# Attention of a two-layer model on one core: the rotation's exchanged half is added by an accumulating DMA, one conditioning gate changes its engine, and the stages of the attention layer stand in another order

## The chip, the core and the metric

The kernel runs on one core of one Trainium2 chip. The core has a matrix engine (TensorE, PE), a vector engine (VectorE, DVE), a scalar engine (ScalarE, ACT), a general engine (GpSimd, POOL) and a sync engine (SyncE, SP), each with its own instruction queue, and 16 DMA engines that serve the queues. The metric is the device time of one execution in microseconds (us).

## The reference

A model of depth 2 with width 1024 and 256 tokens. Layer 0 is an HGRN mixer and a feed-forward block, layer 1 the attention that the change is about and a second feed-forward block. Each of the four blocks is conditioned: shift, scale and gate come from a matrix of the conditioning vector `c`.

```python
mods = einsum('bd,lde->lbe', silu(c), ada_w) + ada_b      # 4 blocks: shift, scale, gate
# layer 1, keys and values of 4 heads, in three branches
k_cmp, v_cmp, k_sel, v_sel, k_win, v_win = split(modulate(x, ...) @ w_kv)
kc = rms_norm(compress(k_cmp)); vc = compress(v_cmp)
ks = apply_rope(rms_norm(k_sel), cos, sin); kw = apply_rope(rms_norm(k_win), cos, sin)
# queries of 16 heads
q = rms_norm(h @ w_q); q_rope = apply_rope(q, cos, sin)
...
o = g0 * softmax(q kc) vc + g1 * softmax(q_rope ks, causal) v_sel + g2 * softmax(q_rope kw, causal) v_win
x = x + gate * (o @ w_out)

def apply_rope(x, cos, sin):
    x1, x2 = split(x, 2)
    return concat([x1 * cos - x2 * sin, x2 * cos + x1 * sin])
```

`apply_rope` is the rotation: each half of a head's 64 values is multiplied by the cosine, and the other half, multiplied by the sine, is subtracted or added.

## The kernel before

Activations stand transposed in SBUF: 128 partitions, 8 chunks of the width, 256 tokens. All is kept in 32-bit floats. Weights come in chunks of 1 MB (`raw<-in_w`, on SP's queue, in the order of one list, into a ring of four buffers). ACT casts a chunk to its high half `wh` (L337), DVE subtracts to get the low half `wl` (L341), and PE multiplies three times, high by high, high by low and low by high (L551 to L553, or two wider matmuls at L563 and L564).

The **conditioning** is computed along the way, piece by piece, in one of two manners. By `ada_pe` PE multiplies the chunk with `c` (L445, tiles `adaps...`), ACT copies, PE transposes (L458, `adat`) and DVE adds the bias. Else DVE multiplies a chunk with `c` and sums it (L406, `junk<-raw,crep`, two instructions to a chunk of 1 MB). The tuple `ON_PE` says which pieces PE takes: `s` for shift and scale, `g` for the gate, the digit for the block. `g2` is the gate of the attention layer, `s3` the shift and scale of the block behind it.

The **attention layer**, `nsa` (L1337), runs from about 354 us to 501 us of the profiled execution. It projects keys and values, then walks a list of tokens, `ORDER["nsa"]`, which says in which order the stages are recorded:

- `c` and `x`: compression of keys and values, softmax of that branch. `K`: the split activations `h` for values and keys. `G`: the three gates `G`. `w`: the values `V` of a branch (PE tile `v`).
- `q0` to `q3`: the projection of four query heads each (PE tile `nq`) and their rotation. `R` and `n`: norms of the keys and the queries, and their factors.
- `s0` to `s7`, `attend_scores` (L1585): for one pair of heads PE computes scores (L1598, `s<-KR,QR`), DVE adds the mask and takes the maximum (L1603, eight instructions, `Pt<-s`), scales it (L1608, `nm`), ACT takes the exponentials with their sums (L485, eight instructions, `Pt`), and DVE forms the factor (L1618, `rs`; `cf`) and multiplies (L1626, `Pt<-Pt,cf`, two instructions).
- `v0` to `v7`, `attend_values` (L1629): PE transposes the pair's `Pt` (L1640, twelve, into `ptt`), ACT (L1645) and DVE (L1643) copy it in four pieces to `PT`, PE multiplies it with `V` (L1658, `po`), and ACT and DVE split the result for the next product (L546, L547).
- `a`: one piece of the conditioning that is due.

A scheduler puts the recorded instructions in an order on each engine by priority. `AHEAD` shifts the priority of a token, `PRI` that of a kind of stage. `PTV` says which of a pair's copies DVE takes, `QACT` and `KACT` are bit masks of the chunks of the queries' and the keys' activations that ACT computes instead of DVE. `Pt` has three buffers, the scores' tiles share four.

The **rotation** is done six times: keys of two branches (`k0`, `k1`) and four groups of queries (`q0` to `q3`; `q0` serves the pairs 0 and 1, and so on). `rotate` (L1260) has POOL issue four DMAs of 32 partitions that copy the raw heads `u` with halves exchanged to `us`, and DVE multiply `u` by gain and cosine into `KR` or `QR` (L1268). Later `rotate_end` (L1272) has DVE multiply `us` by the exchanged gain and the sine (L1277) and add it to `KR` or `QR` (L1279). `us` has two buffers.

Of the kernel before, what the change touches and what calls it, by code (L numbers as in the profile page):

```python
# [21 lines left out]
P = 128  # L22
S = 256
# [10 lines left out]
WIDE = ((3, 5, 6, 7, 9, 10, 11, 12, 13, 14, 15, 16, 17, 18, 19, 20), range(NF))  # L34
ROOTED = [("ffn_in0", 2, 1), ("ffn_in0", 3, 0), ("kv", 2, 0), ("kv", 4, 0), ("ffn_in1", 2, 1), ("ffn_in1", 3, 0)]
PTS = 3
QACT, KACT = 79, 184
CSTK = 7
PTV = 2

AHEAD = {'s4': 5, 'v1': 10, 'G': -10, 'v2': 20, 'v3': 5, 'q3': -40, 'v7': -10, 'v6': 30, 'v5': 5, 'c1': -20, 'v4': 40}
PRI = {'gates': -165, 'av': 10, 'res': 120, 'rot': -90, 'fh': -25}
EPS = 1e-6
NEG = -1e30
LEVELS = (1, 2, 4, 8, 16, 32, 64, 128)
# [11 lines left out]
def _ada_g(l):  # L59
# [11 lines left out]
    "hada": [1, 1, 1, 2, 5, 5, 5, 6, 6, 7, 7, 7],  # L71
    "f0": [6, 6, 7, 10, 11, 11, 13, 13, 15, 18, 19, 22, 23, 23, 25, 27, 28, 28, 32, 33],
    "nsa": (
        "q0 K c0 c1 G w0 q1 R n0 s0 q2 q3 x0 w1 s1 s2 v0 v1 n1 a s3 s4 a v2 a a a v3 a x1 s5 a s6 v4 v6 s7 v5 a a v7 a a a"
    ).split(),
    "f1": [13, 15, 23, 31],
}
# [65 lines left out]
def constants():  # L143
    c = np.zeros((P, NCST), np.float32)

    def put(n, a):
        c[:, CST[n][0]:CST[n][1]] = a.reshape(P, -1)

    put("ident", np.eye(P, dtype=np.float32))
    p = np.arange(P)  # L150
    put("bd64", (p[:, None] // 64 == p[None, :] // 64).astype(np.float32) / 64)
    ex = np.arange(0, 64, 2, dtype=np.float32) / np.float32(64)
    inv = np.float32(1) / np.power(np.float64(10000), ex.astype(np.float64)).astype(np.float32)
    ang = (np.arange(S, dtype=np.float32)[:, None] * inv[None, :]).astype(np.float64)
    put("cos", np.cos(ang).astype(np.float32).T[p % 32])
    put("sin", np.sin(ang).astype(np.float32).T[p % 32] * np.where(p % 64 < 32, -1, 1)[:, None].astype(np.float32))
# [46 lines left out]
class K:  # L203
# [1053 lines left out]
        return u, sq  # L1257

    @first("rot")
    def rotate(self, u, gain, swap, kr, name):  # L1260

        nc = self.nc
        us = self.s2.tile([P, 2, S], F32, tag="us", bufs=2, name=f"us{name}")
        for b in range(4):
            d, e = 32 * b, 32 * (b ^ 1)
            nc.gpsimd.dma_start(us[d:d + 32], u[e:e + 32])
        cs = self.c("cos")[:, None, :].to_broadcast([P, 2, S])
        nc.vector.scalar_tensor_tensor(kr, u, gain, cs, op0=ALU.mult, op1=ALU.mult)  # L1268
        self.swapped.append((kr, us, swap))

    @first("rot")
    def rotate_end(self):  # L1272

        nc = self.nc
        sn = self.c("sin")[:, None, :].to_broadcast([P, 2, S])
        for kr, us, swap in self.swapped:
            r = nc.vector.scalar_tensor_tensor(us, us, swap, sn, op0=ALU.mult, op1=ALU.mult)  # L1277
            self.after(r, self.last_wl)
            nc.vector.tensor_tensor(kr, kr, us, op=ALU.add)  # L1279
# [57 lines left out]
    def nsa(self):  # L1337
        nc = self.nc
        with self.tc.tile_pool(name="ns", bufs=1) as sp, self.tc.tile_pool(name="ns2", bufs=2) as s2, \
                ExitStack() as self.late:  # L1340
            self.sp, self.s2 = sp, s2
            self.swapped = []
# [19 lines left out]
            with ExitStack() as early:  # L1362
# [44 lines left out]
                def values(br):
# [376 lines left out]
```

## Time and profile before

| | |
|---|---|
| median of 3 runs | 712.99 us (712.82 to 713.07) |
| profiled execution | 715.08 us |
| its span, first to last instruction | 713.3 us |
| mean granted TensorE clock | 0.995 of full speed |

The page of the profile gives busy time by engine, the chain of work that ended last (followed back from the last instruction to what released each step), and groups of equal instructions with their count, their busy time and the mean of one in ns. Windows give the same busy times for stretches of the span, with the granted clock (PEclk) and the share in which the DMA engines were busy. In a timeline each row is a run of equal instructions: start, length, engine, line, operation, output and inputs, count, and in brackets how long the engine was idle before it and who ended that.

### The profile page before, as it was taken

Reading aid. Unit: us, or ns where it says so; the run is one execution under the profiler, and the core shown is the slowest. Engines: PE = TensorE matmul, PEld = TensorE weight load, DVE = VectorE, ACT = ScalarE, POOL = GpSimd, SP = SyncE. Lnnn points to the kernel's source line nnn. Section 1 sums busy time; section 2 is a strip of 40 time slices with the busy share of each in tenths; the row PEclk is TensorE's granted clock in tenths of the full one; section 3 lists DMA queues with packets and bytes.
Section 4 is the critical chain, followed back from the end, with each engine's and each line's share of the span. In section 5 each row is a group of like instructions: output and inputs, shape, how many; then the busy total and the mean of one; then the engine's idle time right before and its main releaser. Section 6 shows DMA issues by size and latency. Waiting matters only on the chain.

```text
span 713.3 us, 13972 instructions
## 1 busy us (share of the span) xinstructions
PE 702.6 (99%) x5495; PEld 608.9 (85%) x5495; DVE 583.6 (82%) x1210; ACT 428.5 (60%) x849; POOL 12.2 (2%) x29
## 2 busy tenths in 40 slices
PE   8999999999999999999999999999999999999998
PEld 5998987999988888988998986545899888888887
DVE  6896977799999999999697997667989887686651
ACT  4669977667554665644475656658757655654330
POOL 0000000000000000000002121000000000000000
PEclk9999999999999999999999999989999999999999
DMA  8997768635589998987639643347655766564530
GB/s 356 425 425 293 257 269 305 237 138 182 177 349 345 331 325 305 355 345 279 248 116 338 212 143 134 149 178 262 219 186 188 260 244 220 201 259 155 200 125 23
DMA packets 28067, 174.00 MB, mean 244 GB/s; under 512 B 3297, under 2 KB 4705, under 8 KB 8290
## 3 DMA queue, kind: packets, MB, share of 16 engines
q1 hardware_dynamic: 26800, 170.80, 64.1%
q0 software_dynamic: 768, 1.57, 0.8%
q8 instruction: 43, 0.70, 0.4%
q10 hardware_dynamic: 434, 0.74, 0.3%
q14 instruction: 22, 0.18, 0.1%
HBM read 170.48 MB, written 1.05 MB: 240 GB/s over the span
## 4 chain that ended last, share of the span: by engine, by line
PE 88%; ACT 5%; DVE 4%; DMA 3%; issue 0%; SPq 0%; DVEq 0%
PE ffo L563 11%; PE ff L563 9%; PE ffo L564 6%; PE ff L564 5%; ACT Pt L485 3%; PE ff L551 2%; PE ff L553 2%; PE ff L552 2%; PE nso L563 2%; DMA raw<-in_w 2%; PE po L1658 2%; PE adapsss L445 2%; PE ptt L1640 1%; PE hg_g L551 1%; PE hg_i L993 1%; PE s L1598 1%
## 5 line engine op out<-in xcount | busy, mean ns | idle before, releaser
L341 DVE TENSOR_TENSOR wl<-raw,wh 128x1024 fp32r<-128x1024 f32 x193 | 234.5, 1222 | 50.7 <-ACT wh L337 49.6
L337 ACT CAST wh<-raw 128x1024 fp32r<-128x1024 f32 x193 | 200.0, 1049 | 116.3 <-PE ffo L563 37.0
L563 PE MATMUL ffo<-g,wh 128*128 128x512 f32 x330 | 116.0, 394 | 0.0
L563 PE MATMUL ff<-h,wh 128*128 128x512 f32 x280 | 99.9, 395 | 0.0
L564 PE MATMUL ffo<-g,wl 128*128 128x256 f32 x330 | 93.0, 282 | 0.0
L564 PE MATMUL ff<-h,wl 128*128 128x256 f32 x280 | 78.5, 280 | 0.0
L563 PEld LDWEIGHTS ffo<-g,wh 128*128 128x128 f32 x330 | 62.0, 188 | 14.5
L406 DVE CUSTOM_DVE_ANT_0 junk<-raw,crep 128x1024 f32<-128x1024 f32 x60 | 73.2, 1220 | 0.3 <-DMA raw<-in_w 0.2
L563 PEld LDWEIGHTS ff<-h,wh 128*128 128x128 f32 x280 | 52.8, 189 | 12.1 <-DVE h L740 0.2
L564 PEld LDWEIGHTS ffo<-g,wl 128*128 128x128 f32 x330 | 61.9, 188 | 0.0
L564 PEld LDWEIGHTS ff<-h,wl 128*128 128x128 f32 x280 | 52.8, 189 | 0.2
L552 PE MATMUL ff<-h,wh 128*128 128x258 f32 (+1 forms) x144 | 40.5, 283 | 0.0
L553 PE MATMUL ff<-h,wl 128*128 128x258 f32 (+1 forms) x144 | 40.3, 283 | 0.0
L551 PE MATMUL ff<-h,wh 128*128 128x258 f32 (+1 forms) x144 | 40.2, 284 | 0.0
L485 ACT ACTIVATE Pt<-Pt,nm,rq 128x128 f32<-128x128 f32 x64 | 34.2, 539 | 3.6 <-DVE nm L1608 3.6
L802 DVE SCALAR_TENSOR_TENSOR x<-ffo,mod,x 128x256 f32<-128x256 f32 x31 | 14.9, 482 | 16.6 <-PE ffo L564 11.5
L553 PEld LDWEIGHTS ff<-h,wl 128*128 128x128 f32 x144 | 27.2, 190 | 0.0
L552 PEld LDWEIGHTS ff<-h,wh 128*128 128x128 f32 x144 | 27.2, 189 | 0.0
L551 PEld LDWEIGHTS ff<-h,wh 128*128 128x128 f32 x144 | 26.9, 189 | 0.3
L563 PE MATMUL nso<-h,wh 128*128 128x512 f32 x64 | 22.5, 394 | 0.0
L1603 DVE CUSTOM_DVE_ANT_0 Pt<-s,cst 128x128 f32<-128x128 f32 (+1 forms) x64 | 19.4, 353 | 3.5 <-PE s L1598 3.4
L546 ACT CAST g<-fg 128x256 fp32r<-128x256 f32 x44 | 17.8, 405 | 7.0 <-DVE fg L1209 5.6
(499 smaller groups left out, 1799.5 us busy)
## 6 DMA issues: line engine op xcount, KB each, us to landing
raw<-in_w SPq DMA_DIRECT2D x147, 1024.0 KB, 5.3
raw<-in_w SPq DMA_DIRECT2D x11, 512.0 KB, 6.9
rawq<-in_w SPq DMA_DIRECT2D x3, 1024.0 KB, 9.1
rawv<-in_w SPq DMA_DIRECT2D x2, 1024.0 KB, 11.3
w1late<-in_w SPq DMA_DIRECT2D x2, 1024.0 KB, 9.8
x<-in_x SPq DMA_DIRECT2D x2, 512.0 KB, 4.9
rawv<-in_w SPq DMA_DIRECT2D x2, 512.0 KB, 8.2
out<-x SPq DMA_DIRECT2D x8, 128.0 KB, 1.9
```

The costliest lines, as they stand in the source:

```text
L337: r = nc.scalar.copy(wh, u)
L341: r = nc.vector.tensor_tensor(wl, u, wh.bitcast(F32), op=ALU.subtract)
L406: r = nc.vector.tensor_tensor_reduce(out=junk, in0=t[:, h * D:(h + 1) * D], in1=self.crep, scale=1.0, scalar=0.0, op0=ALU.mult, op1=ALU.ad ...
L485: r = nc.scalar.activation(out, in_, func, **kw)
L546: self.nc.scalar.copy(hi, v)
L551: mm(ps, lhsT=wh, rhs=hh, start=first, stop=False)
L552: mm(ps, lhsT=wh, rhs=hl, start=False, stop=False)
L553: return mm(ps, lhsT=wl, rhs=hh, start=False, stop=last)
L563: mm(ps, lhsT=w[k][0], rhs=b, start=k == 0, stop=False)
L564: mm(ps[:, 0], lhsT=w[k][1], rhs=b[:, 0], start=False, stop=k == n - 1)
L802: nc.vector.scalar_tensor_tensor(xn[:, m], p, gate[:, m:m + 1], xn[:, m], op0=ALU.mult, op1=ALU.add)
L1603: nc.vector.tensor_tensor_reduce(out=Pt[half][:, br, o:o + n], in0=ps[half][:, br], in1=cs[:, S - n:], scale=1.0, scalar=-3e38, op0=ALU.ad ...
```

## The change

Four things are changed.

1. The rotation. DVE multiplies the raw heads by gain and sine into `us` first, and by gain and cosine into `KR` or `QR`; then four accumulating DMAs on POOL's queue add `us`, halves exchanged, to `KR` or `QR`. The addition on DVE and `rotate_end` are gone, and the sign of the sine's table is turned.
2. The gate `g2` leaves `ON_PE`: its conditioning is now computed by DVE.
3. `PTV` goes from 2 to 0, so that all copies of the transposed `Pt` are ACT's; `QACT` leaves ACT three chunks instead of five, `KACT` gives it five instead of four.
4. `ORDER["nsa"]`, `AHEAD` and `PRI` have other entries.

```diff
-QACT, KACT = 79, 184
+QACT, KACT = 84, 217
-PTV = 2
+PTV = 0
-AHEAD = {'s4': 5, 'v1': 10, 'G': -10, ...}
-PRI = {'gates': -165, 'av': 10, 'res': 120, 'rot': -90, 'fh': -25}
+AHEAD = {'q3': -55, 'c1': -55, 'v4': 110, ...}
+PRI = {'gates': -150, 'av': 0, 'res': 195, 'rot': -75, 'fh': -25}
-ON_PE = ("s1", "g0", "g2", "s3")
+ON_PE = ("s1", "g0", "s3")
-        "q0 K c0 c1 G w0 q1 R n0 s0 q2 q3 x0 w1 s1 s2 v0 v1 n1 a s3 s4 ..."
+        "c0 K c1 q0 G w0 R q1 n0 q2 s0 s1 w1 x0 s2 q3 n1 a v0 v1 s3 a s4 ..."
-    put("sin", np.sin(ang)... * np.where(p % 64 < 32, -1, 1)[:, None]...)
+    put("sin", np.sin(ang)... * np.where(p % 64 < 32, 1, -1)[:, None]...)
-    def rotate(self, u, gain, swap, kr, name):
+    def rotate(self, u, gain, kr, name):
         nc = self.nc
+        cs, sn = (self.c(n)[:, None, :].to_broadcast([P, 2, S]) for n in ("cos", "sin"))
         us = self.s2.tile([P, 2, S], F32, tag="us", bufs=2, name=f"us{name}")
+        nc.vector.scalar_tensor_tensor(us, u, gain, sn, op0=ALU.mult, op1=ALU.mult)
+        nc.vector.scalar_tensor_tensor(kr, u, gain, cs, op0=ALU.mult, op1=ALU.mult)
         for b in range(4):
             d, e = 32 * b, 32 * (b ^ 1)
-            nc.gpsimd.dma_start(us[d:d + 32], u[e:e + 32])
-        cs = self.c("cos")[:, None, :].to_broadcast([P, 2, S])
-        nc.vector.scalar_tensor_tensor(kr, u, gain, cs, op0=ALU.mult, op1=ALU.mult)
-        self.swapped.append((kr, us, swap))
-    def rotate_end(self):
-        for kr, us, swap in self.swapped:
-            r = nc.vector.scalar_tensor_tensor(us, us, swap, sn, op0=ALU.mult, op1=ALU.mult)
-            self.after(r, self.last_wl)
-            nc.vector.tensor_tensor(kr, kr, us, op=ALU.add)
+            nc.gpsimd.dma_start(kr[d:d + 32], us[e:e + 32], accum_op=ALU.add)
```

In the changed kernel the lines of this layer stand 11 to 14 lower than before (the product with the cosine is L1266, that with the sine L1265, the DMAs L1269, the maximum L1589, the final product L1612).

The order of instructions moves with it. The first place is DVE at the first query rotation, before, from the product with the cosine on; `wl_0_5116` is the low half of the weights of the second query group, `h_4879` the activations of keys and values.

```order
L1268 SCALAR_TENSOR_TENSOR QR<-huq_4869,cols,cst 128x512 [waits Activation_49]
L547 TENSOR_TENSOR hrt<-hrr,hry 128x256 [waits Activation_49]
L341 TENSOR_TENSOR wl_0_5116<-raw_5011,wh_0_5115 128x1024 [waits DMAHW6_49,PE_49,Activation_49]
L537 TENSOR_SCALAR sg<-cmp_4916 128x256 [waits PE_49]
L547 TENSOR_TENSOR h_4879<-t_4880,h_4879 128x256 [waits DMAHW5_49,DMAHW4_49,Activation_49]
```

And the same place now (`usq_5006` is the first query rotation's `us`, `wl_0_5131` and `h_4847` are the weights and activations of the rows above):

```order
L1266 SCALAR_TENSOR_TENSOR QR<-huq_5002,cols,cst 128x512
L528 TENSOR_SCALAR hrt<-hrt 128x256 [waits DVE_49]
L530 TENSOR_TENSOR hrr<-hrt,hry 128x256 [waits DVE_49]
L547 TENSOR_TENSOR hrt<-hrr,hry 128x256 [waits Activation_49]
L1265 SCALAR_TENSOR_TENSOR usq_5006<-huq_5002,cols,cst 128x512 [waits DMASW4_49,DMASW6_49,DMASW2_49,DMASW0_49]
L341 TENSOR_TENSOR wl_0_5131<-raw_4843,wh_0_5130 128x1024 [waits DMAHW6_49,Activation_49]
L547 TENSOR_TENSOR h_4847<-t_4848,h_4847 128x256 [waits DMAHW5_49,DMAHW4_49,Activation_49]
```

The product into `us` has come in ahead of the weights and the splits. It waits for four DMAs of POOL's queue (the DMASW semaphores): its buffer was that of the first keys, whose four DMAs read it.

The second place is PE at the first scores, before. The pair 0 (`s_5225` to `s_5234`) stands alone; the next scores come 88 rows later.

```order
L1598 MATMUL s_5225<-KR,QR 128x256 [waits DVE_49,PE_49]
L1598 MATMUL s_5226<-KR,QR 128x256
L994 MATMUL v_5421<-wl_0_5423,h_4879 128x256
L995 MATMUL v_5421<-wh_0_5422,h_4879 128x256
L1598 MATMUL s_5233<-KR,QR 128x512 [waits PE_49,Activation_49]
L1598 MATMUL s_5234<-KR,QR 128x512 [waits DVE_49,PE_49]
```

Now the scores of the pairs 0 (`s_5291` to `s_5300`) and 1 (`s_5327` on) follow each other:

```order
L1584 MATMUL s_5291<-KR,QR 128x256 [waits DMASW1_49,DMASW2_49,DMASW0_49,DMASW3_49,DVE_49,PE_49]
L1584 MATMUL s_5292<-KR,QR 128x256 [waits DMASW5_49,DMASW6_49,DMASW4_49,DMASW7_49,DMASW3_49,DMASW2_49]
L1584 MATMUL s_5299<-KR,QR 128x512 [waits PE_49,Activation_49]
L1584 MATMUL s_5300<-KR,QR 128x512 [waits DVE_49,PE_49]
L1584 MATMUL s_5327<-KR,QR 128x256 [waits DVE_49,PE_49]
L1584 MATMUL s_5328<-KR,QR 128x256 [waits DVE_49,PE_49]
```

The scores of pair 1 moved up to pair 0, and the first of them wait for the accumulating DMAs instead of for an addition on DVE.

The third place is DVE between the products of the first pairs, now; `Pt_5290` is pair 0, `Pt_5326` pair 1, `raw_5227` a chunk of the weights of the gate `g2`, `css` and `cmx` belong to the compressed branch.

```order
L1612 TENSOR_TENSOR Pt_5290<-Pt_5290,cf 128x2x384
L406 ISA junk,mod_3748<-raw_5227,crep 128x1024 [waits DMAHW3_49]
L406 ISA mod_3748 128x1
L1604 RECIPROCAL rs<-sm 128x8 [waits Activation_49]
L1559 TENSOR_REDUCE cmx<-css 128x16 [waits Activation_49]
L1608 TENSOR_TENSOR cf<-rs,G 128x4 [waits DVE_49]
L1608 TENSOR_TENSOR cf<-rs,G 128x4x2
L1560 RECIPROCAL cmx<-cmx 128x16 [waits DVE_49]
L1612 TENSOR_TENSOR Pt_5326<-Pt_5326,cf 128x2x384 [waits DVE_49]
```

Before, no reduction of the conditioning (L406) stood on DVE in this layer's attention; now eight do, two ahead of the first pair's maximum and six between it and that of the third-last pair.

More of the change, by code (lines that the diff above doesn't have):

```diff
@@ L36 @@
 PTS = 3
-QACT, KACT = 79, 184
+QACT, KACT = 84, 217
 CSTK = 7
-PTV = 2
-AHEAD = {'s4': 5, 'v1': 10, 'G': -10, 'v2': 20, 'v3': 5, 'q3': -40, 'v7': -10, 'v6': 30, 'v5': 5, 'c1': -20, 'v4': 40}
-PRI = {'gates': -165, 'av': 10, 'res': 120, 'rot': -90, 'fh': -25}
+PTV = 0
+AHEAD = {'q3': -55, 'c1': -55, 'v4': 110, 'c0': -70, 's7': 5, 'x1': -35, 's3': 10, 's2': -5, 's0': 60, 'q0': 80, 'w1': -10, 's4': -80, 'v2': -25, 'K': 75, 'R': 60, 'v5': 20, 'v7': -15, 'G': -5}
+PRI = {'gates': -150, 'av': 0, 'res': 195, 'rot': -75, 'fh': -25}
 EPS = 1e-6
@@ L73 @@
     "nsa": (
-        "q0 K c0 c1 G w0 q1 R n0 s0 q2 q3 x0 w1 s1 s2 v0 v1 n1 a s3 s4 a v2 a a a v3 a x1 s5 a s6 v4 v6 s7 v5 a a v7 a a a"
+        "c0 K c1 q0 G w0 R q1 n0 q2 s0 s1 w1 x0 s2 q3 n1 a v0 v1 s3 a s4 a a v2 v3 a x1 s6 s5 a s7 v4 v6 a v5 a v7 a a a a"
     ).split(),
@@ L155, in constants @@
     put("cos", np.cos(ang).astype(np.float32).T[p % 32])
-    put("sin", np.sin(ang).astype(np.float32).T[p % 32] * np.where(p % 64 < 32, -1, 1)[:, None].astype(np.float32))
+    put("sin", np.sin(ang).astype(np.float32).T[p % 32] * np.where(p % 64 < 32, 1, -1)[:, None].astype(np.float32))
     caus = np.zeros((P, 2, P), np.float32)
@@ L1259, in rotate @@
     @first("rot")
-    def rotate(self, u, gain, swap, kr, name):
+    def rotate(self, u, gain, kr, name):
         nc = self.nc
+        cs, sn = (self.c(n)[:, None, :].to_broadcast([P, 2, S]) for n in ("cos", "sin"))
         us = self.s2.tile([P, 2, S], F32, tag="us", bufs=2, name=f"us{name}")
+        nc.vector.scalar_tensor_tensor(us, u, gain, sn, op0=ALU.mult, op1=ALU.mult)
+        nc.vector.scalar_tensor_tensor(kr, u, gain, cs, op0=ALU.mult, op1=ALU.mult)
         for b in range(4):
             d, e = 32 * b, 32 * (b ^ 1)
-            nc.gpsimd.dma_start(us[d:d + 32], u[e:e + 32])
-        cs = self.c("cos")[:, None, :].to_broadcast([P, 2, S])
-        nc.vector.scalar_tensor_tensor(kr, u, gain, cs, op0=ALU.mult, op1=ALU.mult)
-        self.swapped.append((kr, us, swap))
-    @first("rot")
-    def rotate_end(self):
-        nc = self.nc
-        sn = self.c("sin")[:, None, :].to_broadcast([P, 2, S])
-        for kr, us, swap in self.swapped:
-            r = nc.vector.scalar_tensor_tensor(us, us, swap, sn, op0=ALU.mult, op1=ALU.mult)
-            self.after(r, self.last_wl)
-            nc.vector.tensor_tensor(kr, kr, us, op=ALU.add)
-        self.swapped = []
+            nc.gpsimd.dma_start(kr[d:d + 32], us[e:e + 32], accum_op=ALU.add)
     def head_sums(self, pairs):
@@ L1327, in head_mul @@
         nc = self.nc
-        self.rotate_end()
         for i in range(len(pairs)):
@@ L1341, in nsa @@
             self.sp, self.s2 = sp, s2
-            self.swapped = []
             self.PC, self.Pt, self.RQ, self.rq = {}, {}, {}, None
@@ L1384, in nsa @@
                 for br in range(2):
-                    self.rotate(kk[br][0], self.col("k_norm", 1 + br), self.col("k_swap", 1 + br), KR[:, :, br], f"k{br}")
+                    self.rotate(kk[br][0], self.col("k_norm", 1 + br), KR[:, :, br], f"k{br}")
                 ks = [KR[:, :, br] for br in range(2)]
@@ L1398, in query @@
                     qq[i] = self.raw_heads(proj("nq", i, hq), f"q{i}", qd[0][:, i % 2] if i > 1 else None)
-                    self.rotate(qq[i][0], self.col("q_norm"), self.col("q_swap"), self.QR[:, 2 * i:2 * i + 2], f"q{i}")
+                    self.rotate(qq[i][0], self.col("q_norm"), self.QR[:, 2 * i:2 * i + 2], f"q{i}")
                 def query_norm(g):
@@ L1403, in query_norm @@
                     self.QN[g] = [u for u, _ in pairs]
-                    self.rotate_end()
                     self.row_norm(pairs, g)
```

## The prediction

> **What bounds the kernel now.** I read the page first, for the share of each engine and the chain that ended last.
>
> ```profile
> span 713.3 us, 13972 instructions
> PE 702.6 (99%) x5495; PEld 608.9 (85%) x5495; DVE 583.6 (82%) x1210; ACT 428.5 (60%) x849; POOL 12.2 (2%) x29
> PE 88%; ACT 5%; DVE 4%; DMA 3%; issue 0%; SPq 0%; DVEq 0%
> ```
>
> TensorE (PE) carries 88% of the chain; the 12% that other engines carry is the room. The diff begins at the keys' rotation (about 374 us) and ends with the attention layer, so I cut that part with the windows view.
>
> ```profile
> core 0: us, PE busy (x) PEld busy (x) DVE busy (x) ACT busy (x) POOL busy (x), PEclk, DMA share, GB/s
> 392.00:418.50 26.50, 26.42 (x218) 24.74 (x217) 24.76 (x48) 17.40 (x36) 5.88 (x12) 1.00 0.62 219
> 418.50:432.60 14.10, 14.10 (x113) 12.99 (x112) 11.98 (x44) 5.85 (x21) 0.00 (x0) 1.00 0.26 85
> 432.60:450.40 17.80, 17.48 (x151) 9.87 (x148) 12.70 (x52) 12.87 (x43) 1.96 (x4) 1.00 0.53 194
> 450.40:473.20 22.80, 20.47 (x134) 12.21 (x134) 15.13 (x65) 13.40 (x46) 0.00 (x0) 0.85 0.15 53
> 473.20:499.60 26.40, 25.64 (x190) 13.43 (x188) 19.09 (x76) 21.01 (x65) 0.00 (x0) 1.00 0.76 296
> ```
>
> Of 392 to 418.5, PE is busy for 26.42 of 26.50 us: a delay there is not absorbed. From 450.4 to 473.2 it is busy for 20.47 of 22.80 us, at a granted clock of 0.85. Finer windows show where that clock went, and the timeline of PE what came first.
>
> ```profile
> 460.00:465.00 5.00, 2.70 (x21) 2.17 (x20) 4.70 (x12) 5.00 (x21) 0.00 (x0) 0.87 0.53 206
> 465.00:470.00 5.00, 4.97 (x25) 3.32 (x25) 2.90 (x8) 1.78 (x5) 0.00 (x0) 0.50 0.01 3
> 461.96 1.39 PE L1640 MATMUL ptt<-cst,Pt 128*128 128x128 f32 x9 [0.62 <-DVE Pt L1626]
> 465.03 0.90 PE L1640 MATMUL ptt<-cst,Pt 128*128 128x128 f32 x3 [1.68 <-ACT PT L1645]
> ```
>
> PE waits 0.62 us for a product of DVE and 1.68 us for a copy of ACT, and the next 5 us run at half clock. So this middle is bound by the softmax loop of scores (PE), maximum (DVE), exponential (ACT), product (DVE), transposes (PE), copies (ACT). DVE is busy for 11.98 + 12.70 + 15.13 = 39.8 us of the 54.7 between 418.5 and 473.2 and waits for 14.9. The rows behind most of that:
>
> ```profile
> 418.62 0.28 DVE L1603 CUSTOM_DVE_ANT_0 Pt<-s,cst 128x128 f32<-128x128 f32 x1
> 439.84 0.20 DVE L1618 RECIPROCAL rs<-sm 128x8 f32<-128x8 f32 x1 [1.53 <-ACT Pt L485]
> 449.79 0.42 DVE L547 TENSOR_TENSOR h<-po,h 128x256 fp32r<-128x256 f32 x1 [2.53 <-ACT h L546]
> 460.13 0.20 DVE L1618 RECIPROCAL rs<-sm 128x8 f32<-128x8 f32 x1 [2.00 <-ACT Pt L485]
> 469.57 0.42 DVE L547 TENSOR_TENSOR h<-po,h 128x256 fp32r<-128x256 f32 x1 [2.06 <-ACT h L546]
> 473.24 0.29 DVE L1603 CUSTOM_DVE_ANT_0 Pt<-s,cst 128x128 f32<-128x128 f32 x1 [0.20 <-PE s L1598]
> ```
>
> DVE starts the first pair's maximum at 418.62 and the third-last pair's at 473.24; in between it stands still because one pair's exponentials or copies are not done and nothing else is queued ahead.
>
> **The rotation of the keys.** These rows set the cost of the new wait.
>
> ```profile
> 379.76 1.41 DVE L1268 SCALAR_TENSOR_TENSOR KR<-huk,cols,cst 128x512 f32<-128x512 f32 x2
> 386.77 0.42 DVE L547 TENSOR_TENSOR hrt<-hrr,hry 128x256 fp32r<-128x256 f32 x1
> 391.53 1.23 DVE L341 TENSOR_TENSOR wl<-raw,wh 128x1024 fp32r<-128x1024 f32 x1 [4.33 <-ACT wh L337]
> L1266 POOL DMA_DIRECT2D usk<-huk x8: 496/497/628, 374.3 to 381.0; - x8
> DMA to landing us min/median/max: 5.6/6.2/7.0
> DMA to landing us min/median/max: 1.9/2.5/3.1
> ```
>
> (The first landing row is that of the keys' copies, in a stretch full of weight loads; the second is that of the queries' copies, later.) Today the copies depend only on the raw heads. In the changed kernel they come behind DVE's two products, and the third rotation's `us` takes the first one's buffer, so its product on DVE waits for the first keys' four accumulating DMAs. Queued behind it on DVE are the low half of the next query weights (`wl`) and the splits of `h` that PE needs for the values at about 392. Today DVE idles 4.33 us there, until 391.53, and that hides part. The products end at 379.76 + 1.41, plus two more products of 0.70 (1.4) and a neighbour of 0.42 that now stands ahead, so at 383.0. The two keys' DMAs alternate on POOL's queue, so the last of the four is the seventh issue: 7 x 0.497 = 3.5, 386.5. With the keys' landing row, 6.2, it lands at 392.7; the product itself (0.7) ends at 393.4, **1.9 us** behind 391.53. The trace has no accumulating DMA. From below, the queries' 2.5 us gives 0, since the wait then ends inside the idle time; from above, two passes of 6.2 give 12.4 and 8.0 us. I take 6.2, because the transfers are the same 64 KB out of and into SBUF in the same loaded stretch. Below nothing I exclude, since at 391.53 DVE waits for ACT anyway.
>
> A page weighs against that. The Trainium skill, "Collectives: The Full Stack", section "The bandwidth ceiling: the fold count and why AG ≠ RS ≠ AR", says that a DMA that adds needs two reads for each write, and that such a step moved half of what a copying step moved. No row here shows it; by it the landing is nearer to 12.4 and the sum below becomes 714.0. That lies between the second and the third rival, and its chance is in theirs.
>
> **The rest of the rotation.** Six additions on DVE go, and the product with the sine stays.
>
> ```profile
> L1277 DVE SCALAR_TENSOR_TENSOR usq<-usq,cols,cst 128x512 f32<-128x512 f32 x4 | 3.0, 748 | 0.0
> L1279 DVE TENSOR_TENSOR QR<-QR,usq 128x512 f32<-128x512 f32 x4 | 2.8, 688 | 0.0
> ```
>
> That is 6 x 0.69 = 4.1 us of DVE. In 392 to 418.5, by the order of both kernels, two conditioning reductions (2.4), one weight split (1.2) and two early products (1.45) come in, two of the keys' products (1.5) and four additions (2.75) leave: 0.8 us more, into DVE's 1.7 us of slack there, so nothing. The queries' DMAs have 5 us and more before the first scores that read them; at 2.5 us they hide, and if one took 6.2 it would cost about 1.
>
> **The second mixing gate, the copies, the order.**
>
> ```profile
> L445 PE MATMUL adapsg<-raw,c 128*32 128x256 f32 x64 | 4.3, 382 | 0.0
> L406 DVE CUSTOM_DVE_ANT_0 junk<-raw,crep 128x1024 f32<-128x1024 f32 x60 | 73.2, 1220 | 0.3 <-DMA raw<-in_w 0.2
> L1643 DVE COPY PT<-ptt 128x384 f32<-128x384 f32 x8 | 4.4, 552 | 0.0
> L1645 ACT COPY PT<-ptt 128x384 f32<-128x384 f32 x24 | 10.7, 478 | 13.4 <-PE ptt L1640 11.7 <-PE po L1658 1.4
> ```
>
> PE loses 4.3 us of matmuls, DVE gains 8 reductions of 1.22 (9.8 us), and 8 copies go from DVE (4.4 us) to ACT (8 x 0.48 = 3.8). I count between the same two marks, first maximum of the first pair to first maximum of the third-last. There the order gives DVE six of the reductions (+7.3), four copies fewer (-2.2), four rotation steps fewer (-2.9) and one product fewer (-0.95): 39.8 + 1.3 = 41.1 us. The waits were 14.9. A reduction that stands where DVE waited takes its own length out of the wait: 14.9 - 7.3 = 7.6. So the stretch is 48.7 us instead of 54.7, **-6.0**. I take that because one stands right behind the first pair's product and ahead of the second's sums, two behind the second's product, three ahead of the fourth pair's maxima, where the waits of 1.53 to 2.53 us are; and because the changed order computes two pairs' scores ahead of any exponential, so ACT goes from one to the other. The bounds: if all waits re-form, 41.1 + 14.9 gives +1.3; if they fall to 4.9, which is what remains when I walk the changed order with these durations, -8.7.
>
> PE must be able to follow. Between the marks it gives up 4.3 us, idles for 0.00 + 0.32 + 2.33 = 2.65 and loses 3.4 to the clock (0.15 x 22.8), against some 3.3 us of the third shift's matmuls that are moved there: 7 us, enough for 6. Its 4.3 us are not credited again, since most of them run while PE would wait for exponentials. What is late next is PE itself.
>
> **The tail.**
>
> ```profile
> 494.96 1.83 DVE L1626 TENSOR_TENSOR Pt<-Pt,cf 128x768 f32<-128x768 f32 x2
> ```
>
> From 473.2 to the last product's end (496.8) are 23.6 us; the walk gives 21.6, because those third-shift matmuls have left. Half is credited, **-1.0**: the four copies that go to ACT there, busy for 21.01 of 26.40 already, may cost up to 4 x 0.48 = 1.9, so the bounds are +1.9 and -2.0. Behind it PE is the only bound:
>
> ```profile
> 505.00:600.00 95.00, 94.80 (x589) 85.01 (x588) 84.81 (x156) 60.47 (x111) 0.00 (x0) 1.00 0.60 218
> 600.00:700.00 100.00, 100.00 (x573) 87.59 (x572) 65.22 (x95) 46.53 (x71) 0.00 (x0) 1.00 0.49 179
> ```
>
> It runs there without gaps at full clock, on work that the change leaves alone, so what is won or lost by then reaches the end.
>
> **The sum.** +1.9 - 6.0 - 1.0 = -5.1. The profiled execution takes 715.08 (span 713.3, 1.78 around it), 2.09 above the median of the runs, 712.99; the terms are differences, so the same shift holds, 715.08 - 5.1 = 710.0 profiled and **707.9** for the median.
>
> **Rivals.** First, all pays: the new wait costs 0 and the walk holds, -8.7 - 2.0 = -10.7, capped by PE's own account of 392 to 499.6 (idle 3.5, clock 3.4, matmuls 4.3: 11.2). That gives 702.3. For it: the queries' 2.5 us; against it: every wait would have to go.
>
> Second, the waits take new places: ACT has the eight copies and two consecutive pairs' exponentials, so products come later, and the order moves stalls instead of removing them. At -1.9 from the stretch against +1.9 from the new wait it is 713.0, no change. For it: ACT is busy for 21.01 of the tail's 26.40 us; against it: only 5.85 of 14.10 and 12.87 of 17.80 before.
>
> Third, slower: the accumulating DMAs land late. Above 4.4 us each further microsecond delays `wl`, `h` and then a full PE one for one, so from 12.8 us on (a wait of 8.4, against 7.0 won and the 1.4 below) the kernel is slower; at three passes, 18.6 us, the wait costs 14.2 and the time is 720.2. For it: an addition needs the target's old value as well, and the rows it lands in are pieces of 256 elements; against it: 64 KB is small against the 1 MB that lands in 5.3 us. That the exchange would still need its additions on DVE is excluded by the order.
>
> A second page bears on the stall. The Trainium skill, "TensorE: Matmul & The Clock Gate", section "What's actually happening", gives two clocks, full and half, the half after an idle window of about 3.4 us. The trace agrees on the half (0.50 behind the stalls) but shows it after 2.70 busy of 5.0 us, not after pure idling; by the rule as it stands shorter waits could not cost the clock, and were the 3.4 us to come back with waits that sum up alike, the time would be 711.3, at the edge of the second rival.
>
> **Chances.** The forecast with its neighbours (705 to 711.5) 0.57, all pays 0.16, no change 0.13, slower 0.14. A measurement of this kernel can tell about 0.2% from no change, 1.4 us. The range runs from 703 to 715: it leaves out half of the first rival and most of the third. Faster 0.73, same 0.13, slower 0.14.
>
> **What would show it.** The wait in front of the third rotation's product on DVE should be about 4 us, and the `wl` behind it 2 us later than today. The accumulating DMAs' landing is to be read at the keys: 6 confirms, 12 and more is the third rival. The time from the first to the third-last maximum should be 49 us with DVE's waits near 8, and the half clock near 465 gone; if DVE waits there as long as today, the second rival holds. The last product should come 22 to 23 us after the third-last maximum. Wrong altogether would be a PE that is not full in 392 to 418.5 or behind 505, since then the terms do not add up to the end.

## The result, and the profile after

The changed kernel is **slower** by 0.5%: 716.97 us (median of 4 runs, 716.71 to 717.08) against 713.03 us (712.82 to 713.67), a ratio of 1.0053 with a 95% interval of 1.0036 to 1.0071. The forecast was 707.9 us, and 716.97 lies outside its range of 703 to 715.

The profiled executions are 715.08 us before and 716.71 us after (spans 713.3 and 714.9). The kernel before varies more than its first runs showed: in the later series it lay between 712.1 and 715.8 us, with granted clocks of 0.994 to 1.000 (712.1 to 712.6 us where the clock was 1.000). Its profiled execution, with 0.995, is one of the longer ones, so the spans differ by only 1.6 us where the medians differ by 3.9. The page of the changed kernel begins:

```profile
span 714.9 us, 13853 instructions
PE 696.8 (97%) x5429; PEld 608.1 (85%) x5429; DVE 585.5 (82%) x1216; ACT 429.6 (60%) x855; POOL 20.0 (3%) x29
PE 93%; DVE 3%; DMA 2%; ACT 1%; issue 0%; POOL 0%; DVEq 0%; POOLq 0%
```

PE is busy for 5.8 us less than before (696.8 against 702.6) and yet the span is longer: PE stands still for 18 us in all, before for 11. Three marks, which both kernels have, show where. The numbers are from the timelines, the lengths behind them are differences. The prediction shows the first two marks of before; the fence has the three of now and the third of before.

```profile
429.13 0.28 DVE L1589 CUSTOM_DVE_ANT_0 Pt<-s,cst 128x128 f32<-128x128 f32 x1
475.22 0.28 DVE L1589 CUSTOM_DVE_ANT_0 Pt<-s,cst 128x128 f32<-128x128 f32 x1
524.72 0.28 PE L551 MATMUL ff<-h,wh 128*128 128x258 f32 x1
522.96 0.28 PE L551 MATMUL ff<-h,wh 128*128 128x258 f32 x1
```

| mark | before | after | length up to it, before | after |
|---|---|---|---|---|
| first pair's first maximum (DVE) | 418.62 | 429.13 | 418.62 | 429.13 (+10.5) |
| third-last pair's first maximum (DVE) | 473.24 | 475.22 | 54.6 | 46.1 (-8.5) |
| first matmul of the second feed-forward block (PE) | 522.96 | 524.72 | 49.7 | 49.5 (-0.2) |

Behind the third mark both take the same time. So the middle gained more than forecast, and the part ahead of the first maximum lost 10.5 us. The windows of the changed kernel show that part (columns as in the prediction):

```profile
376.00:392.00 16.00, 15.26 (x126) 13.04 (x124) 11.58 (x21) 9.69 (x20) 7.05 (x8) 1.00 0.95 305
392.00:400.40 8.40, 0.02 (x1) 0.03 (x1) 2.30 (x4) 0.00 (x0) 1.26 (x3) 0.76 0.81 285
400.40:406.60 6.20, 6.20 (x29) 6.20 (x30) 5.35 (x12) 4.78 (x13) 1.91 (x3) 0.50 0.42 42
406.60:429.00 22.40, 22.39 (x187) 21.23 (x186) 17.81 (x35) 11.82 (x22) 5.46 (x8) 1.00 0.53 163
```

From 392 to 400.4 us PE does nothing (0.02 of 8.40 us), ACT nothing, and then PE runs for 6.2 us at a clock of 0.50. The timelines of POOL, DVE and PE, and the landing times of the keys' DMAs, say why:

```profile
382.21 7.05 POOL L1269 DMA_DIRECT2D KR<-usk  x8 [31.10 <-DVE KR L1266]
398.10 0.75 DVE L1265 SCALAR_TENSOR_TENSOR usq<-huq,cols,cst 128x512 f32<-128x512 f32 x1 [9.89 <-DMA KR<-usk]
398.77 1.22 DVE L341 TENSOR_TENSOR wl<-raw,wh 128x1024 fp32r<-128x1024 f32 x1
400.38 0.58 PE L995 MATMUL v<-wh,h 128*128 128x256 f32 x1 [8.56 <-DVE h L547]
L1269 POOL DMA_DIRECT2D KR<-usk x8: 995/1996/3144, 382.2 to 386.1; - x8
DMA to landing us min/median/max: 2.7/9.4/13.6
```

It is the wait that the prediction named, at the place that it named: the first query rotation's product on DVE (L1265) waits 9.89 us for the first keys' accumulating DMAs, the weight split `wl` and the splits of `h` stand behind it, and PE waits 8.56 us for `h`. The product ends at 398.8 us; forecast was 393.4. What was wrong is the size: the DMAs were taken to land 6.2 us behind their issue, and took 9.4 in the median and up to 13.6. The one that the product waits for, the last of the first keys' four, took 12.4 us.

In the second and third part the work of DVE and its waits are these (windows between the marks, before and then after; busy times of PE, PEld, DVE and ACT behind the length):

```profile
418.62:473.24 54.62, 51.97 (x390) 34.99 (x392) 39.72 (x162) 32.00 (x109) 1.96 (x4) 0.94 0.30 107
```

```profile
429.13:475.22 46.09, 45.42 (x338) 30.84 (x338) 40.45 (x165) 32.25 (x110) 3.88 (x5) 1.00 0.57 192
```

DVE works 0.7 us more (40.45 against 39.72) and waits 5.6 us instead of 14.9, and the clock is whole (1.00 against 0.94, which is 3.3 us of 54.6). These 3.3 us belong to the profiled execution of the kernel before; its executions with a mean clock of 1.000 did not lose them.

### The profile page after: what moved, and what is told of

Same layout as the page of the kernel before. It is cut to its first block, busy times and chain, and to the rows that moved or that the text cites. A ratio compares the mean times of both kernels' runs of the same rounds, so it can differ in the third digit from the quotient of the medians.

```text
span 714.9 us, 13853 instructions
## 1 busy us (share of the span) xinstructions
PE 696.8 (97%) x5429; PEld 608.1 (85%) x5429; DVE 585.5 (82%) x1216; ACT 429.6 (60%) x855; POOL 20.0 (3%) x29
## 4 chain that ended last, share of the span: by engine, by line
PE 93%; DVE 3%; DMA 2%; ACT 1%; issue 0%; POOL 0%; DVEq 0%; POOLq 0%
PE ffo L563 11%; PE ff L563 9%; PE ffo L564 5%; PE ff L564 5%; PE po L1644 3%; PE ff L551 2%; PE ff L552 2%; PE ff L553 2%; PE s L1584 2%; PE adapsss L445 2%; PE nso L563 2%; PE ptt L1626 2%; DMA KR<-usk 2%; PE hg_g L551 1%; PE hg_i L993 1%; PE hgo L551 1%
## 5 line engine op out<-in xcount | busy, mean ns | idle before, releaser
L341 DVE TENSOR_TENSOR wl<-raw,wh 128x1024 fp32r<-128x1024 f32 x193 | 233.8, 1219 | 52.5 <-ACT wh L337 51.7
L406 DVE CUSTOM_DVE_ANT_0 junk<-raw,crep 128x1024 f32<-128x1024 f32 x68 | 82.7, 1216 | 0.1
L802 DVE SCALAR_TENSOR_TENSOR x<-ffo,mod,x 128x256 f32<-128x256 f32 x31 | 14.9, 481 | 16.6 <-PE ffo L564 11.5
L1589 DVE CUSTOM_DVE_ANT_0 Pt<-s,cst 128x128 f32<-128x128 f32 (+1 forms) x64 | 19.5, 353 | 2.6 <-PE s L1584 2.4
```

The source lines that it names most:

```text
L341: r = nc.vector.tensor_tensor(wl, u, wh.bitcast(F32), op=ALU.subtract)
L406: r = nc.vector.tensor_tensor_reduce(out=junk, in0=t[:, h * D:(h + 1) * D], in1=self.crep, scale=1.0, scalar=0.0, op0=ALU.mult, op1=ALU.ad ...
L1589: nc.vector.tensor_tensor_reduce(out=Pt[half][:, br, o:o + n], in0=ps[half][:, br], in1=cs[:, S - n:], scale=1.0, scalar=-3e38, op0=ALU.ad ...
```

## The experiments

Theory A: the loss is the wait for the first keys' DMAs, with the half clock behind it. Theory B: the loss comes from the gate on DVE, the copies on ACT or the new order. Each ratio below is to the kernel before, in the runs of the same series.

### Is the wait the loss?

**A buffer of its own for the first keys' product.** It lies in another pool than the two that take turns.

```diff
-        us = self.s2.tile([P, 2, S], F32, tag="us", bufs=2, name=f"us{name}")
+        if us is None:
+            us = self.s2.tile([P, 2, S], F32, tag="us", bufs=2, name=f"us{name}")
...
-                    self.rotate(kk[br][0], self.col("k_norm", 1 + br), KR[:, :, br], f"k{br}")
+                    self.rotate(kk[br][0], self.col("k_norm", 1 + br), KR[:, :, br], f"k{br}",
+                                sk.tile([P, 2, S], F32, name="usk") if br == 0 else None)
```

> The first keys' product with the sine gets a buffer of its own, so that the first query rotation no longer waits for the keys' accumulating DMAs. Theory A (the loss is that wait: 9.89 us on DVE, behind which PE stands for 8.56 us and then runs 6.2 us at half clock, together some 10.5 us up to the first maximum): no wait of over 1 us in front of that product, PE not at half clock behind 400 us, and 716.97 - 10.5 = 706.5 us, between 705 and 709. Theory B (the loss is in the gate on DVE, the copies on ACT and the new order): 714 us or more, although the wait is gone.

Measured: 706.69 us (706.03 to 708.01), ratio 0.9902 (0.9876 to 0.9929). In the timeline of DVE the product now stands at 385.82, with no wait ahead of it, and the first and third-last maximum follow at 418.38 and 465.52, 47.1 us apart. The windows that were empty before are full, and the clock is whole:

```profile
385.82 0.75 DVE L1266 SCALAR_TENSOR_TENSOR usq<-huq,cols,cst 128x512 f32<-128x512 f32 x1
418.38 0.29 DVE L1591 CUSTOM_DVE_ANT_0 Pt<-s,cst 128x128 f32<-128x128 f32 x1 [0.46 <-PE s L1586]
465.52 0.29 DVE L1591 CUSTOM_DVE_ANT_0 Pt<-s,cst 128x128 f32<-128x128 f32 x1
DMA to landing us min/median/max: 2.7/9.0/13.4
392.00:400.40 8.40, 8.27 (x68) 8.12 (x68) 7.64 (x19) 5.83 (x14) 0.77 (x1) 1.00 1.08 332
400.40:406.60 6.20, 6.20 (x55) 6.09 (x54) 4.50 (x9) 3.52 (x7) 0.00 (x0) 1.00 0.37 154
```

The DMAs land as late as ever (9.0 in the median, up to 13.4 us), but nobody is queued behind them. The step from 716.97 to 706.69 is 10.3 us; Theory A had said 10.5. Theory B falls.

**The new rotation alone** in the kernel before, with two buffers (`e6`) and with the buffer of its own (`e6b`). All else is as before.

```diff
-            nc.gpsimd.dma_start(us[d:d + 32], u[e:e + 32])
+            nc.gpsimd.dma_start(kr[d:d + 32], us[e:e + 32], accum_op=ALU.add)
...
-                    self.rotate_end()
```

> The kernel before with the new rotation alone (gate on PE, copies, masks, order and priorities as before). Theory A (the third rotation's product waits for the first keys' accumulating DMAs, whatever stands around it): the same wait of 8 to 10 us on DVE near 388 us and PE at half clock behind it, so 713.8 + 8 to 10.5, less up to 4 for the additions that leave DVE: 718 to 724 us. Theory B (the rotation is not what loses): 713 us or less.

> The kernel before with the new rotation alone, and a buffer of its own for the first keys' product. If the 8.5 us that the middle stretch (first to third-last maximum) gained come from the rotation, which no longer holds DVE up: 705 to 709 us. If they come from the gate and the order: 711 to 714 us.

Measured: 723.90 us (ratio 1.0141, 1.0121 to 1.0161) and 716.57 us (1.0038, 1.0026 to 1.0050). The timeline of DVE in the first of them:

```profile
396.56 0.75 DVE L1265 SCALAR_TENSOR_TENSOR usq<-huq,cols,cst 128x512 f32<-128x512 f32 x1 [8.53 <-DMA KR<-usk]
```

The wait is there whatever stands around it, and costs 7.3 us here. The second kernel says something else: without the wait, the rotation alone is still 0.4% slower than the old one; why was not tested. Its middle stretch, between the first and the third-last pair's maximum, is 56.0 us long, so the 8.5 us that the middle gained do not come from the rotation alone:

```profile
418.73 0.28 DVE L1591 CUSTOM_DVE_ANT_0 Pt<-s,cst 128x128 f32<-128x128 f32 x1
474.72 0.29 DVE L1591 CUSTOM_DVE_ANT_0 Pt<-s,cst 128x128 f32<-128x128 f32 x1 [0.20 <-PE s L1586]
```

It was expected at 705 to 709 or at 711 to 714 us, and 716.6 is neither.

**The first keys' four DMAs ahead of the second keys' four**, with two buffers:

```diff
                 for br in range(2):
-                    self.rotate(kk[br][0], ...)
+                    with self.tc.high_priority(offset=-30) if br else ExitStack():
+                        self.rotate(kk[br][0], ...)
```

> The changed kernel with two buffers, but the four accumulating DMAs of the first keys stand ahead of the second keys' four on POOL's queue instead of alternating with them. If the DMAs add one after the other, about 1.7 us apart, the wait for the first keys is over when the fourth of eight has landed, near 392.8 instead of 398 us: a wait of about 5 us in place of 9.9 and 710 to 713 us. If the landing is late for all alike (the weight loads hold up the queue): about 717 us.

Measured: 712.72 us (ratio 0.9980, 0.9969 to 0.9991).

```profile
391.99 0.75 DVE L1265 SCALAR_TENSOR_TENSOR usq<-huq,cols,cst 128x512 f32<-128x512 f32 x1 [5.00 <-DMA KR<-usk]
DMA to landing us min/median/max: 2.7/9.1/13.4
```

All eight land as late as before, but the four that matter are the first ones, and the wait is 5.00 us, as expected of DMAs that finish one after the other. So the alternating order on POOL's queue alone had cost 4 to 5 us (by the medians, and by the ratios).

### Why do these DMAs land late?

Three kernels, all with the wait in place and engines in the changed kernel's order: copies instead of additions (which leaves the sum with the other half out), rows of 2 KB instead of two pieces of 1 KB, and both.

Without the addition (`e2`, `e14`):

```diff
-            nc.gpsimd.dma_start(kr[d:d + 32], us[e:e + 32], accum_op=ALU.add)
+            nc.gpsimd.dma_start(kr[d:d + 32], us[e:e + 32])
```

In whole rows (`e3`, `e14`):

```diff
-            KR = sp.tile([P, 2, 2, S], F32, name="KR")
+            KR = sp.tile([P, 2, 2, S], F32, name="KR").rearrange("p b g s -> p g b s")
```

> The rotation's DMAs copy instead of adding, so the sum with the other half is left out; the same instructions in the same order, pieces and buffers. If the addition makes the DMAs late (A1): the keys' DMAs land as the copies of the kernel before did, about 6 us behind their issue instead of 9.4 (median) and up to 13.6, the wait in front of the first query product falls from 9.9 to about 4 us, and the time is 708 to 711 us. If the pieces of 1 KB (A2) or the weight loads beside them (A3) do it: landings as now, about 1.7 us apart, and 717 us.

> KR is stored with the branch ahead of the group, so that an accumulating DMA of the keys writes rows of 2 KB instead of two pieces of 1 KB; engines' orders are the same. If the pieces make the DMAs late (A2): landings 0.8 us apart like those of the queries, the fourth of the first keys at about 392 us, a wait of about 4 us and 709 to 711 us. If it is the addition itself (A1) or the weight loads (A3): landings about 1.7 us apart as now, and 717 us, within 1 us.

> The changed kernel with both DMA properties changed: copies instead of additions, so the sum with the other half is left out, and rows of 2 KB. The last of the first keys' four landed 12.4 us behind its issue in the changed kernel, 8.0 as a copy in pieces of 1 KB, 10.8 as an addition in rows of 2 KB. If addition and pieces each bring a share of their own: about 6.4 us, a wait of about 4 us and 708.5 to 711 us. If the weight loads beside them set a floor: 8 us as with the copies in pieces, and 711 us.

The rows for the keys' DMAs on POOL (duration of an issue, min/median/max ns) and their landing, of the copies in pieces, the additions in whole rows and the copies in whole rows, in this order:

```profile
L1269 POOL DMA_DIRECT2D KR<-usk x8: 533/536/673, 382.0 to 385.8; - x8
DMA to landing us min/median/max: 2.0/6.7/8.4
```

```profile
L1269 POOL DMA_DIRECT2D KR<-usk x8: 908/1811/2837, 382.2 to 385.8; - x8
DMA to landing us min/median/max: 2.6/9.3/11.6
```

```profile
L1269 POOL DMA_DIRECT2D KR<-usk x8: 498/498/631, 382.6 to 386.1; - x8
DMA to landing us min/median/max: 1.9/6.6/7.3
```

| | longest landing | wait on DVE | time, ratio (interval) |
|---|---|---|---|
| add, 1 KB (the changed kernel) | 13.6 | 9.89 | 716.97, 1.0053 (1.0036 to 1.0071) |
| add, 2 KB | 11.6 | 8.00 | 713.91, 1.0000 (0.9988 to 1.0012) |
| copy, 1 KB | 8.4 | 5.46 | 710.98, 0.9959 (0.9947 to 0.9971) |
| copy, 2 KB | 7.3 | 3.84 | 710.67, 0.9959 (0.9944 to 0.9974) |

The addition makes the wait 4.2 to 4.4 us longer (8.00 - 3.84, 9.89 - 5.46), the small pieces 1.6 to 1.9 us. What is left with neither, 6.6 us in the median, is what the prediction had taken from the kernel before (6.2). So there is a floor of that size, and the addition is the larger part of the rest. That the weight loads beside them set the floor is likely, but no run took the loads away: the queries' DMAs, most of them later, landed in 2.5 us in the median as copies (before) and in 3.2 as additions (now), and the DMA engines' busy share in the changed kernel is 0.95 from 376 to 392 us and 0.53 from 406.6 to 429.

The Trainium skill, "Collectives: The Full Stack", section "The bandwidth ceiling: the fold count and why AG ≠ RS ≠ AR", has the adding step of a collective read two operands for each write and move half of what a copying step moves. The trace agrees in direction; the factor between the longest landings is 1.6 here (11.6 to 7.3, 13.6 to 8.4), with the floor in both.

The last two rows have nearly the same median with waits of 5.46 and 3.84 us. Their runs overlap (710.2 to 712.4 and 710.1 to 711.8 us), and the profiled executions, from which the waits are, are 1.25 us apart (712.35 and 711.10), so the medians alone do not say that the length of the wait hardly counts. The traces say what does. In both copies PE's clock went to 0.50 from 396 to 400 us; in those with whole rows PE had stood for only 2.52 us ahead of that:

```profile
394.79 0.58 PE L995 MATMUL v<-wh,h 128*128 128x256 f32 x1 [2.52 <-DVE h L547]
396.00:400.00 4.00, 4.00 (x21) 4.00 (x20) 3.43 (x7) 3.89 (x12) 0.00 (x0) 0.50 0.78 286
423.50 0.28 DVE L1589 CUSTOM_DVE_ANT_0 Pt<-s,cst 128x128 f32<-128x128 f32 x1
```

The same rows of PE and of the first maximum in the copies in pieces, and then in the additions in whole rows:

```profile
395.76 0.58 PE L995 MATMUL v<-wh,h 128*128 128x256 f32 x1 [3.46 <-DVE h L547]
424.49 0.28 DVE L1589 CUSTOM_DVE_ANT_0 Pt<-s,cst 128x128 f32<-128x128 f32 x1
```

```profile
398.55 0.58 PE L995 MATMUL v<-wh,h 128*128 128x256 f32 x1 [6.57 <-DVE h L547]
427.12 0.28 DVE L1589 CUSTOM_DVE_ANT_0 Pt<-s,cst 128x128 f32<-128x128 f32 x1
```

In the four kernels PE stands for 2.52, 3.46, 6.57 and 8.56 us. Against `e1_own_buffer`, whose first maximum is at 418.38, theirs comes 5.1, 6.1, 8.7 and 10.75 us later: each time PE's standstill and another 2.2 to 2.7 us. That rest goes with the half clock, since behind each standstill PE runs some 6 us at 0.50 (6.1, 6.1, 5.8 and 6.2), which loses 3. So the wait has two prices: its own length, and 2 to 3 us that are nearly the same for a short wait and a long one.

### Where does the rest come from?

**The old rotation in the changed kernel:**

```diff
-            nc.gpsimd.dma_start(kr[d:d + 32], us[e:e + 32], accum_op=ALU.add)
+            nc.gpsimd.dma_start(us[d:d + 32], u[e:e + 32])
...
+                    self.rotate_end()
```

> The rotation of the kernel before in the changed kernel; gate, copies, masks, order and priorities as changed. Theory A: the rest of the change gains what the windows show, 8.5 us from the first to the third-last pair's maximum in the profiled executions and 0 to 1 us more behind, so 704 to 709 us. Theory B: 713 us or more, since what loses is still in.

Measured: 719.02 us (ratio 1.0063, 1.0043 to 1.0084), outside what Theory A expected and within what Theory B expected. It does not speak for Theory B, because the old form makes waits of its own in this order. The timeline of DVE:

```profile
396.30 0.75 DVE L1277 SCALAR_TENSOR_TENSOR usq<-usq,cols,cst 128x512 f32<-128x512 f32 x1 [4.34 <-DMA usq<-huq]
449.99 0.75 DVE L1277 SCALAR_TENSOR_TENSOR usq<-usq,cols,cst 128x512 f32<-128x512 f32 x1 [5.59 <-DMA usq<-qd]
```

In the old form DVE has work behind the DMA, and this order puts it right behind; in the new form the first reader behind the DMA is a matmul on PE, later.

**Order and priorities of before**, all else as in `e1_own_buffer`; `e9` has all three lines of the diff, `e15` the first two, `e16` the last one:

```diff
-AHEAD = {'q3': -55, 'c1': -55, 'v4': 110, ...}
+AHEAD = {'s4': 5, 'v1': 10, 'G': -10, ...}
-PRI = {'gates': -150, 'av': 0, 'res': 195, 'rot': -75, 'fh': -25}
+PRI = {'gates': -165, 'av': 10, 'res': 120, 'rot': -90, 'fh': -25}
-        "c0 K c1 q0 G w0 R q1 n0 q2 s0 s1 ..."
+        "q0 K c0 c1 G w0 q1 R n0 s0 q2 q3 ..."
```

> As e1_own_buffer (706.7 us), but with the list of tokens, AHEAD and PRI of the kernel before. If the order makes the middle stretch shorter (two pairs' scores ahead of any exponential): 710 to 714 us. If the rotation and the gate do it alone: 706 to 708 us.

> As e1_own_buffer (706.7 us), but AHEAD and PRI are those of the kernel before; the list of tokens is the new one, so that the scores of the pairs 0 and 1 stand together. If the list makes the middle stretch short: 706 to 709 us. If the tuned priorities do it: 712 to 716 us, as with e9_old_order (715.6 us).

> As e1_own_buffer (706.7 us), but the list of tokens is that of the kernel before, with the new AHEAD and PRI. If the list makes the middle stretch short: 712 to 716 us. If the priorities do it: 706 to 709 us.

Measured: 715.57 us (ratio 1.0021, 1.0008 to 1.0034), 719.13 us (1.0081, 1.0066 to 1.0096) and 725.55 us (1.0161, 1.0113 to 1.0209). The last of these varied most, from 721.2 to 728.5 us. With the old list and the old priorities the middle stretch is 54.7 us, and up to the first matmul of the second feed-forward block it is 104.17 us, here and, in the last row, in `e1_own_buffer`:

```profile
418.08:472.74 54.66, 54.34 (x381) 33.70 (x380) 43.66 (x171) 35.07 (x114) 6.29 (x8) 1.00 0.62 217
418.08:522.25 104.17, 100.14 (x648) 67.32 (x645) 82.79 (x281) 73.99 (x205) 6.29 (x8) 0.97 0.52 185
418.38:514.06 95.68, 94.78 (x640) 64.33 (x639) 79.58 (x277) 71.53 (x204) 6.12 (x8) 1.00 0.54 191
```

The stretch up to that matmul was 104.3 us in the kernel before (54.62 + 49.72). So with the gate's reductions on DVE and the additions gone it is not shorter, and the new order, with them, makes it 95.7. The middle alone says less, because the old order fills it here with other work: PE is busy for 54.34 of its 54.66 us, and its waits and the half clock come behind. Over the whole, PE stands for 4.0 us against 0.9 with the new order, and the clock is 0.97 against 1.00. List and priorities only work together: each alone in the other's company is slower than both old or both new. For neither of the two had that been expected; both lie above all ranges named for them.

**The gate on PE again:**

```diff
-ON_PE = ("s1", "g0", "s3")
+ON_PE = ("s1", "g0", "g2", "s3")
```

> As e1_own_buffer (706.7 us), but the second mixing gate's conditioning is on PE again. If the reductions on DVE fill waits and PE's matmuls were on the path: up to 4.3 us more, 709 to 712 us. If PE did them while it waited anyway, as I credited: 706 to 708 us.

Measured: 739.52 us (ratio 1.0358, 1.0313 to 1.0404), far from both expectations. The group of these matmuls here and three rows of PE's timeline; in the second fence, PE's row in the kernel before:

```profile
L445 PE MATMUL adapsg<-raw,c 128*32 128x256 f32 x64 | 22.9, 444 | 0.0
443.62 0.62 PE L445 MATMUL adapsg<-raw,c 128*32 128x256 f32 x2
444.17 0.39 PE L553 MATMUL nq<-h,wl 128*128 128x256 f32 x1
444.49 0.62 PE L445 MATMUL adapsg<-raw,c 128*32 128x256 f32 x2
```

```profile
439.45 3.64 PE L445 MATMUL adapsg<-raw,c 128*32 128x256 f32 x58
```

The order puts the gate's matmuls two by two between those of a projection, and so a pair and one projection matmul take 0.87 us (443.62 to 444.49). In the kernel before 58 of them in a row took 3.64 us, 0.06 each. The 64 take 22.9 us instead of 4.3. So this run is no measure of the gate's move; it shows that the changed order does not fit a gate on PE. What the move is worth by itself stays open; together with copies and masks, in the old order, it is 716.57 to 715.57 us, 1 us (`e6b` to `e9`, runs of one series), and the intervals of their ratios overlap.

**One copy per pair on DVE again:** in `e1_own_buffer`.

```diff
-PTV = 0
+PTV = 2
```

> As e1_own_buffer (706.7 us), but PTV is 2 again, so DVE takes one of each pair's four copies. I credited the move nothing of its own: 705 to 708 us. If the copies on ACT hold the exponentials up, it is faster than 705 us; if DVE is the tighter of the two, 709 us or more.

Measured: 711.07 us (ratio 0.9950, 0.9934 to 0.9967). That is the range named for the case that DVE is the tighter of the two. The move of the copies, which the forecast credited with nothing, is worth 3 to 4 us in this order (by the ratios and by the medians): the middle is 51.7 us instead of 47.1.

```profile
419.18:470.83 51.65, 50.93 (x351) 32.75 (x350) 42.18 (x169) 30.92 (x105) 6.29 (x8) 0.97 0.59 207
```

**Shortened reductions** of the second gate, in `e1_own_buffer`:

```diff
+            w = 32 if l == 2 and kind != "ada_ss" else D
-            r = nc.vector.tensor_tensor_reduce(out=junk, in0=t[:, h * D:(h + 1) * D], in1=self.crep, ...)
+            r = nc.vector.tensor_tensor_reduce(out=junk[:, :w], in0=t[:, h * D:h * D + w], in1=self.crep[:, :w], ...)
```

> As e1_own_buffer (706.7 us), but the eight reductions of the second mixing gate on DVE take 32 of 1024 columns, so most of that gate's conditioning is left out: some 9 us less work on DVE, and the scheduler's order shifts a little. If the reductions fill waits, as I held for six of them: 704.5 to 707.5 us. If they stand on the path: 698 to 702 us.

Measured: 708.99 us (ratio 0.9921, 0.9906 to 0.9936), above the first range and far from the second. Some 8 us less work on DVE bring nothing. So the reductions are not on the path, as the forecast held. That the time is even higher may come from an order that shifted with the edit; it was not tested.

**Own buffer and whole rows together**, the edits of `e1` and `e3`:

> As e1_own_buffer (706.7 us), and KR stored so that the keys' DMAs write rows of 2 KB. The keys' DMAs land 1 to 2 us earlier, but nothing waits for them any more: 706 to 707.5 us. If the traffic of the small pieces held up the weight loads: 705 us or less.

Measured: 707.16 us (ratio 0.9899, 0.9885 to 0.9914), no different from `e1_own_buffer`. Where nobody waits for the DMAs, how they are cut does not matter.

`e1_own_buffer` and `e10_own_buffer_whole_rows` beat both kernels, by 1.0% the one before.

## Why the prediction was wrong

**The new wait, +1.9: wrong in size, and this decides.** Place, cause and the queue behind it were right, and so was the start of the DMAs (first issue at 382.21, forecast 383.0). The step that failed is "With the keys' landing row, 6.2": the duration of a copying DMA stood for an adding one. The DMA that the product waited for took 12.4 us. The 2 by 2 table shows 6.6 us for copies in whole rows, as taken, and some 6 us more of wait for additions in pieces (9.89 against 3.84). The upper bound of the unknown, two passes or 12.4 us, was what came; the prediction had weighed it and kept it out of the sum. Taken at 12.4, the same sum gave 714.0, still 3 us short.

**The half clock behind the wait: missing from the sum.** The prediction passed a wait on one for one. One run shows this step by itself: in `e14_copy_whole_rows` the product ends at 393.3 us, as forecast (393.4), and yet the kernel takes 710.67 us, 4.0 more than with no wait in `e1_own_buffer`, where the prediction had 1.9. In the changed kernel the product ended 7.3 us later than the `wl` before began (398.8 against 391.53), but the first maximum came 10.5 us later. The window behind the wait shows the rest: 6.2 us at a clock of 0.50, 3.1 us lost. The profile of before had shown the same thing in another place (0.50 behind two waits), and I had priced it there, but not behind my own wait. The sign that the prediction called wrong altogether came with it: from 392 to 400.4 us PE was busy for 0.02 of 8.40 us.

The Trainium skill, "TensorE: Matmul & The Clock Gate", section "What's actually happening", has the clock halved by an idle window of about 3.4 us. The 8.56 us here agree with it, while 2.52 us in `e14_copy_whole_rows` were enough too.

**The third rival** was thereby the right case, with a chance of 0.14 and its point of decision set too high (12.8 us): with the clock in the price, it lies lower.

**The middle stretch, -6.0: right in sign and near in size, with a wrong reason.** It was -8.5 between the marks, 3.3 of it from a half clock that not every execution of the kernel before has; DVE's work was 40.45 us (forecast 41.1) and its waits 5.6 (7.6). The forecast let the six reductions take their length out of the waits, and passed on the 6.0 us of other work that leaves DVE. The reductions do cost nothing (`e13_short_reductions`), but with the old order the work that has left brings nothing (`e9_old_order`, 104.2 us up to the feed-forward block, as before). List and priorities together make it short, and the copies on ACT are worth 3 to 4 us (`e8_copies_on_dve`), where nothing had been credited. How the order does it, in which of its moves, was not tested.

**The tail, -1.0:** to the last product's end, where it was counted, 22.0 us instead of 23.6; -0.2 up to the feed-forward block. Both lie within its bounds.

**The sum without the wait.** -6.0 - 1.0 = -7.0 was forecast for all else; `e1_own_buffer`, which has all else and no wait, is 713.79 - 706.69 = 7.1 us faster than the kernel before in the same series. That the two agree is partly luck, since their parts differ. So 8.4 of the 9.1 us by which the forecast missed are the wait's: 1.9 forecast, 10.3 measured between `e1_own_buffer` and the changed kernel.

## What to carry to other kernels

A transfer that takes over an engine's work has a landing time of its own: take it from an adding DMA if it adds, count the issues ahead of it on its queue, and look for the first instruction that needs its *source* buffer back, not only its result. A wait that leaves PE idle for several microseconds also costs the microseconds at half clock behind it (here 2.2 to 2.7 us, whether PE stood for 2.5 or 8.6). Lists and priorities that were tuned together are undone together: with half of them, or with one piece of work on another engine, the kernel may be slower than with neither.

## What had not been expected of the hardware

- An issue of an adding DMA on POOL lasts 995 to 3144 ns in the trace, of a copying one with the same pieces 533 to 673 ns, though the issues start equally far apart (about 0.55 us: eight from 382.2 to 386.1).
- With the weight loads beside them, eight adding DMAs of 64 KB, issued within 4 us, landed up to 13.6 us behind their issue, the copying ones up to 8.4 us (both in pieces of 1 KB).
- Matmuls of 32 columns that alternate in pairs with matmuls of 128 columns took 0.87 us per pair and neighbour, and 0.06 us each in a row of 58.
- The stretches of half clock ahead of a kernel's end lasted 3.41, 6.83, 10.24 or 13.65 us in all traces here, steps of 3.41: 10.24 in the changed kernel (from 396.3), 6.83 in both copies, 6.83 in the kernel before.
